# Input projections of a hybrid attention and GLA layer by a seven-product scheme, with attention and GLA as side work

## The chip, the core and the metric

The kernel runs on one core of a Trainium2 chip. A core has a matrix engine (TensorE, PE in the profile; its weight loads are listed as PEld), a vector engine (VectorE, DVE), a scalar engine (ScalarE, ACT), a general engine (GpSimd, POOL) and a queue engine that issues transfers (SyncE, SP). Each engine works through its own instructions in order and waits on semaphores for the others. The metric is device time in microseconds from the first to the last instruction of one execution, with inputs and outputs in device memory (DRAM).

## What is computed

One layer of a decoder on 2048 prompt tokens and 8 x 8 new tokens (2112 in all), 1024 wide, in single precision. One input matrix gives eleven projections. Sliding-window attention (blocks of 128 tokens, each seeing itself and the block before) and a gated linear attention (GLA, 4 heads, a recurrent state carried from chunk to chunk) are computed from them, gated, projected and merged; an output projection and a layer normalisation follow. Cut to its core:

```python
z = jnp.einsum('btd,dn->btn', x, w_in)
q, k, v, g_att, gq, gk, gv, g_gla, g_lr, r_att, r_gla = jnp.split(z, SPLIT_POINTS, axis=-1)
o_att = swa_prompt(q, k, v, attn_sink, rel_table)          # or swa_sample, with the caches
log_a = log_sigmoid(g_lr @ w_gk_up + b_gk) / 16
o_gla, S = gla(gq * HK ** -0.5, gk, gv, log_a, s0)         # per chunk, with b = cumsum(log_a):
    # S = exp(b_last) * S + (k * exp(b_last - b)).T @ v
    # o = (q * exp(b)) @ S_before + causal((q * exp(b)) @ (k * exp(-b)).T) @ v
o_gla = o_gla * rsqrt(mean(o_gla ** 2) + EPS) * gla_norm_w
h_att = (o_att * silu(g_att)) @ w_pa
h_gla = (o_gla * silu(g_gla)) @ w_pg
y = (sigmoid(r_att) * h_att + sigmoid(r_gla) * h_gla) @ w_o
x = layer_norm(DN_ALPHA * x + y, ln_g, ln_b)
```

The widths of the projections are q 512, k 128, v 128, g_att 512, gq 512, gk 512, gv 1024, g_gla 1024, g_lr 16, r_att 1024, r_gla 1024. Outputs besides x are the last keys and values and the GLA states.

## The kernel before

Every large product runs at near single precision as three matmuls of a faster operand type: both factors are split into a high part (a rounded copy, made by ACT) and a low part (the remainder, by default made by DVE), and high x high, high x low and low x high are summed in PSUM. `split`, lines 114 to 118, is this pair of instructions; its lines 115 and 116 stand for nearly all splits in the profile.

The kernel has four stages.

1. *Attention*, six chunks of tokens (`CHUNKS`: four of 384, one of 256, one of 256 + 64 samples). For each chunk the ten 128-column tiles of k, v, q and g_att are projected by `proj` (lines 176 to 187, eight slices of the 1024-wide sum by three matmuls, the chunk's tokens streaming), the 16 gate columns by lines 638 and 639. The x tiles are split once per chunk (`part_x`; from the second chunk on, POOL makes every second low part). Attention of the blocks of the chunk runs as side work: functions are put into a list of time slots with `at`, and `tick`, called after each projection, runs those of the next slot (`att_scores`, `att_trans`, `att_out`). The results go to `ua_d` in DRAM.
2. *GLA*, four heads by the same six chunks. x is loaded and split again for each head. k, q and the two gate tiles go through `proj`, the values through `proj_t` (lines 189 to 200, x stationary, 256 value columns streaming, so that the values come out with tokens on the partitions). `gla_z`, `gla_a`, `gla_b`, `gla_c` are the side work of a block of 128 tokens, placed by `chain`. Sums of x tiles that the later passes need ("combinations", `combine_load` and `combine_do`, four additions each) are made here too.
3. *Four passes* by a seven-product scheme (Strassen's in Winograd's form): `w_pa`, `w_ra`, `w_rg`, `w_pg`. A pass treats its product as a 2 x 2 block product (two halves of the sum, and pairs of 352-token groups and of 128-column tiles), with seven block products in place of eight (`ORDER`, `combine`). A *unit* is one of the seven products for one of three token pairs (`MS`); a *group* is a unit's 128-column tile `p`, twelve matmuls of 352 columns (six in w_pa), lines 1276 to 1278. `prep_w` makes sums of weight tiles on POOL and splits them; `prep_x` splits the x sums, 1408 wide; `combine` adds the product to the accumulators on DVE (lines 1123 to 1140), with one addition on POOL (line 1130); a sink stores the finished tile. Nothing else runs beside these passes except the last combinations and early loads of w_o.
4. *Output projection and layer norm* (`Rows`), tiles of 128 tokens.

The order on PE is the order of the program text. The other engines' instructions are put in order by a planner that ranks them by program order and modelled readiness. Tiles come from pools of fixed numbers of buffers; PSUM has three banks `pd` for projections and five `pa` for side work and for the passes.

Of the kernel before, what the change touches and what calls it, by code (L numbers as in the profile page):

```python
# [21 lines left out]
P = 128  # L22
# [19 lines left out]
CHUNKS = [(0, 384), (384, 384), (768, 384), (1152, 384), (1536, 256), (1792, 320)]  # L42
# [4 lines left out]
NU = 29  # L47
NX = 20
# [3 lines left out]
def kernel(ctx, tc, io):  # L52
# [4 lines left out]
    phase = ctx.enter_context(ExitStack())  # L57
    sb = phase.enter_context(tc.tile_pool(name="sb", bufs=1, reuse_waits="tile"))
# [3 lines left out]
    ctx.enter_context(tc.manual_schedule(engines={mybir.EngineType.PE}))  # L62

# [8 lines left out]
    def wtile(dt=F32, name="w"):  # L72
        return sb.tile([P, D], dt, tag="w", name=name, bufs=26)

    def stile(name):
        return sb.tile([P, D], F32, tag="s", name=name, bufs=2)

    def unit(dt=F32, name="u"):
        return sb.tile([P, TM], dt, tag="u", name=name, bufs=NU)

    def small(shape, name, bufs=3):
        return sb.tile(shape, F32, tag=name, name=name, bufs=bufs)

    ua_d = dram.tile([P, 4, NT], F32, name="ua_d")
# [35 lines left out]
    wseq = [0, 10]  # L120
    wready = deque()
    pin = {}

    def wload(n=1):
        for _ in range(n):
            i = wseq[0]
            if i >= wseq[1]:
                return
            wseq[0] += 1
            st = sb.tile([P, D], F32, tag="wst", name="wst", bufs=2)  # L130
            pin["w"] = nc.sync.dma_start(st, io["wt"][i])
            hi = wtile(F32R, "wh")
            lo = wtile(F32R, "wl")
            split(hi, lo, st)
            wready.append((hi, lo))

    def wget():
        if not wready:
            wload()
        return wready.popleft()  # L140

    def xnew():
        return sb.tile([P, TM], F32R, tag="x", name="x", bufs=NX)

    def xstage():
        return sb.tile([P, TM], F32, tag="xst", name="xst", bufs=4)

    def fetch(src, k, t0, T, stage=xstage):
        st = stage()
        nc.sync.dma_start(st[:, :T], src[:, k, t0:t0 + T])  # L150
        return st, T

    def part(f, new=xnew, eng=nc.vector, samples=False):
        st, T = f
        hi, lo = new(), new()
        split(hi[:, :T], lo[:, :T], st[:, :T], eng)
        if samples:
            nc.gpsimd.tensor_copy(hi[:, T:T + NS], lo[:, T - NS:T])
        return hi, lo

    def load_split(src, k, t0, T, new):
        return part(fetch(src, k, t0, T), new)

    def fetch_x(src, t0, T):

        return [fetch(src, k, t0, T, unit if k < KT // 2 else xstage) for k in range(KT)]

    def part_x(fs, share=False, samples=False):

        return [part(f, eng=nc.gpsimd if share and k % 2 else nc.vector, samples=samples)  # L170
                for k, f in enumerate(fs)]

    def load_x(src, t0, T, stage=xstage, samples=False):
        return [part(fetch(src, k, t0, T, stage), samples=samples) for k in range(KT)]

    def proj(ps, w, x, T, mid=False):

        hi, lo = w
        n = len(x)
        for k in range(n):  # L180
            if mid and k == n // 2:
                tick()
            s = slice(k * P, (k + 1) * P)
            xh, xl = x[k]
            mm(ps, hi[:, s], xh[:, :T], start=(k == 0), stop=False)  # L185
            mm(ps, hi[:, s], xl[:, :T], start=False, stop=False)  # L186
            mm(ps, lo[:, s], xh[:, :T], start=False, stop=(k == n - 1))  # L187

    def proj_t(ps, x, c0, n, w, N, cs=slice(None)):

        per = D // N
        for k in range(KT):
            hi, lo = w[k // per]
            r = slice((k % per) * N, (k % per + 1) * N)
            hi, lo = hi[:, r][:, cs], lo[:, r][:, cs]
            xh, xl = x[k]
            xs = slice(c0, c0 + n)
            mm(ps, xh[:, xs], hi, start=(k == 0), stop=False)  # L198
            mm(ps, xl[:, xs], hi, start=False, stop=False)  # L199
            mm(ps, xh[:, xs], lo, start=False, stop=(k == KT - 1))  # L200

    def proj_s(ps, dst, x, c0, w, N, cs=slice(None)):


        per = D // N
        for k in range(KT):
            hi, lo = w[k // per]
            r = slice((k % per) * N, (k % per + 1) * N)
# [324 lines left out]
    def wcap(n):  # L533
        wseq[1] = n
# [381 lines left out]
    for h in range(GH):  # L916
        W2 = {}
        wcap(16 + 6 * h)
        for c, (t0, T) in enumerate(CHUNKS):
# [81 lines left out]
            x = xn  # L1001

# [482 lines left out]
```

## Time and profile before

| what | value |
|---|---|
| median of 3 runs | 1837.22 us (1836.84 to 1837.51) |
| profiled execution, its span | 1836.5 us |
| profiled execution, its own time around the span | not given by the page |
| PE, PEld, DVE, ACT, POOL busy | 98%, 94%, 70%, 46%, 23% of the span |
| mean granted TensorE clock | 0.994 |
| memory read, written | 229.05 MB, 86.14 MB; 172 GB/s over the span |

The profile of one execution says how long each engine was busy, groups instructions by program line with their mean duration, and follows the chain of work that ended last. Matmuls overlap in the array and their ends are modelled, so the mean duration of a matmul is longer than the interval at which matmuls follow each other; the interval is read from start times. A timeline row gives start, duration, engine, line, operation, output and inputs, and a count where like instructions were merged. A row of a stretch gives its length and then, for each engine, busy time and the number of instructions.

### The profile page before, as it was taken

To read this page: it belongs to the slowest core of one execution; us is meant where nothing else is said; L and a number is where in the kernel's file an instruction comes from. 1 tells how busy PE (TensorE), PEld (TensorE's weight loads), DVE (VectorE), ACT (ScalarE), POOL (GpSimd) and SP (SyncE) were. 2 spreads that over 40 slices of the span, in tenths; PEclk is the share of its full clock that TensorE was granted. 3 is DMA by queue.
4 is the path that set the end of the run, shared out by engine and by line. 5 is a ranking of instruction groups with operands and counts; after the bars stand their busy time and mean duration, and the time that the engine had idled before them with its cause. 6 is when DMAs were issued, how large, how long until landed. Compare 5 with 4: busy or idle time off the path is not lost.

```text
span 1836.5 us, 32287 instructions
## 1 busy us (share of the span) xinstructions
PE 1805.2 (98%) x11683; PEld 1718.5 (94%) x11683; DVE 1282.0 (70%) x2663; ACT 850.2 (46%) x1948; POOL 421.9 (23%) x559
## 2 busy tenths in 40 slices
PE   8999999999999999999999999999999999999997
PEld 7988988899999999999999989999999999988886
DVE  6686778767776776777667669748756576966655
ACT  5444545645665664656555553444543443220110
POOL 3310111300110111011110233430355163631111
PEclk9999999999999999999999999999999999999998
DMA  7111013544345444533543189858887967884531
GB/s 243 54 56 38 13 46 100 166 132 156 122 149 168 141 140 153 187 127 112 168 158 122 57 267 316 296 185 281 284 311 256 340 221 265 287 305 142 169 115 41
DMA packets 199408, 316.34 MB, mean 172 GB/s; under 512 B 20797, under 2 KB 161045, under 8 KB 199232
## 3 DMA queue, kind: packets, MB, share of 16 engines
q1 hardware_dynamic: 193536, 306.57, 50.9%
q0 software_dynamic: 5616, 7.58, 1.5%
q8 instruction: 92, 1.51, 0.3%
q14 instruction: 68, 0.56, 0.1%
q10 hardware_dynamic: 96, 0.13, 0.0%
HBM read 229.05 MB, written 86.14 MB: 172 GB/s over the span
## 4 chain that ended last, share of the span: by engine, by line
PE 91%; DMA 2%; DVE 2%; issue 2%; POOL 1%; ACT 1%; SPq 0%; DVEq 0%; POOLq 0%; ACTq 0%
PE pd L185 11%; PE pd L187 11%; PE pd L186 11%; PE pa L1276 9%; PE pa L1278 9%; PE pa L1277 9%; PE pd L199 7%; PE pd L200 7%; PE pd L198 7%; PE pa L421 2%; PE pa L406 1%; PE pa L754 1%; PE pa L755 1%; PE pa L753 1%; POOL a L1159 1%
## 5 line engine op out<-in xcount | busy, mean ns | idle before, releaser
L185 PE MATMUL pd<-x,wh 128*128 128x384 f32 (+2 forms) x1248 | 409.7, 328 | 5.6 <-ACT x L115 5.6
L186 PE MATMUL pd<-x,wh 128*128 128x384 f32 (+2 forms) x1248 | 404.2, 324 | 0.4 <-POOL x L116 0.2
L187 PE MATMUL pd<-x,wl 128*128 128x384 f32 (+2 forms) x1248 | 403.5, 323 | 0.6 <-DVE wl L116 0.6
L1277 PE MATMUL pa<-xl,wh 128*128 128x352 f32 x1168 | 376.1, 322 | 3.6 <-DVE xl L116 3.3
L1276 PE MATMUL pa<-xh,wh 128*128 128x352 f32 x1168 | 377.1, 323 | 0.9 <-ACT a L1120 0.9
L1278 PE MATMUL pa<-xh,wl 128*128 128x352 f32 x1168 | 376.5, 322 | 0.0
L185 PEld LDWEIGHTS pd<-x,wh 128*128 128x128 f32 x1248 | 236.7, 190 | 15.6 <-issue 8.9
L186 PEld LDWEIGHTS pd<-x,wh 128*128 128x128 f32 x1248 | 236.9, 190 | 1.9 <-DVE x L116 1.4
L187 PEld LDWEIGHTS pd<-x,wl 128*128 128x128 f32 x1248 | 236.6, 190 | 1.0 <-DVE wl L116 1.0
L1277 PEld LDWEIGHTS pa<-xl,wh 128*128 128x128 f32 x1168 | 219.4, 188 | 6.1 <-DVE xl L116 6.1
L1276 PEld LDWEIGHTS pa<-xh,wh 128*128 128x128 f32 x1168 | 219.0, 187 | 2.1 <-ACT a L1120 1.1
L1278 PEld LDWEIGHTS pa<-xh,wl 128*128 128x128 f32 x1168 | 220.9, 189 | 0.0
L116 DVE TENSOR_TENSOR xl<-xs,xh 128x1408 fp32r<-128x1408 f32 x63 | 111.4, 1769 | 73.1 <-ACT xh L115 42.8
L198 PE MATMUL pd<-wh,x 128*128 128x256 f32 x512 | 147.8, 289 | 0.0
L199 PE MATMUL pd<-wh,x 128*128 128x256 f32 x512 | 145.6, 284 | 0.6 <-POOL x L116 0.3
L200 PE MATMUL pd<-wl,x 128*128 128x256 f32 x512 | 144.6, 282 | 0.0
L115 ACT CAST x<-xst 128x384 fp32r<-128x384 f32 (+2 forms) x164 | 77.5, 484 | 143.4 <-PE pd L199 112.3
L115 ACT CAST xh<-xs 128x1408 fp32r<-128x1408 f32 x63 | 86.5, 1373 | 98.5 <-PE pa L1278 80.9
L746 POOL TENSOR_SCALAR sq<-sq 128x1 f32<-128x1 f32 (+1 forms) x68 | 21.7, 319 | 467.2 <-ACT ring L745 467.1
L198 PE MATMUL pd<-woh,x 128*128 128x512 f32 x256 | 102.1, 399 | 4.2 <-ACT x L115 4.2
L199 PE MATMUL pd<-woh,x 128*128 128x512 f32 x256 | 102.3, 400 | 0.2 <-DVE x L116 0.2
L200 PE MATMUL pd<-wol,x 128*128 128x512 f32 x256 | 102.0, 398 | 0.0
(345 smaller groups left out, 3695.4 us busy)
## 6 DMA issues: line engine op xcount, KB each, us to landing
wst<-wt SPq DMA_DIRECT2D x33, 512.0 KB, 3.6
xs<-xc_d SPq DMA_DIRECT2D x24, 704.0 KB, 5.7
u<-xT SPq DMA_DIRECT2D x84, 192.0 KB, 4.0
xst<-xT SPq DMA_DIRECT2D x76, 192.0 KB, 2.7
xs<-xT SPq DMA_DIRECT2D x18, 704.0 KB, 6.2
ws<-w_ra SPq DMA_DIRECT2D x36, 256.0 KB, 4.4
ws<-w_rg SPq DMA_DIRECT2D x36, 256.0 KB, 5.1
ws<-w_pg SPq DMA_DIRECT2D x36, 256.0 KB, 5.1
```

The lines of the kernel that those rows point to most:

```text
L115: pin["a"] = nc.scalar.copy(dst_h, src)
L116: i = eng.tensor_tensor(dst_l, src, dst_h.bitcast(F32), ALU.subtract)
L185: mm(ps, hi[:, s], xh[:, :T], start=(k == 0), stop=False)
L186: mm(ps, hi[:, s], xl[:, :T], start=False, stop=False)
L187: mm(ps, lo[:, s], xh[:, :T], start=False, stop=(k == n - 1))
L198: mm(ps, xh[:, xs], hi, start=(k == 0), stop=False)
L199: mm(ps, xl[:, xs], hi, start=False, stop=False)
L200: mm(ps, xh[:, xs], lo, start=False, stop=(k == KT - 1))
L421: mm(ot[pr, :], vb[:, pr], A["pT", bi, kv][:, hf], start=(hf == h0), stop=(hf == 1))
L1276: mm(ps, wh[:, ks], xh[:, ts], start=(k == 0), stop=False)
L1277: mm(ps, wh[:, ks], xl[:, ts], start=False, stop=False)
L1278: mm(ps, wl[:, ks], xh[:, ts], start=False, stop=(k == q.kh - 1))
```

## The change

Stages 1 to 3 become one list of eight seven-product passes over all 2112 tokens: attention (`w_at`, five pairs of column tiles, so five groups a unit), three GLA passes (`w_g0` to `w_g2`, together k and q, values and gates of the four heads, four groups a unit), then `w_pa`, `w_ra`, `w_rg`, `w_pg` as before. Every projection is written to DRAM by a sink (`z_kv`, `z_q`, `z_ga`, `z_kq`, `z_vv`, `z_gg`; the gates after their silu). Attention and GLA read them back and run as side work of later passes: attention in chunks of 256 tokens beside the first GLA pass, one block in five ticks; the GLA chains of the four heads one after another from the second GLA pass to twelve ticks before `w_pg`. A tick follows every group (every second one in `w_pa`). The combinations of x move into the attention pass, together with the product for the 16 gate columns, now from unsplit tiles in four 32-column tiles of PE. In the GLA passes the low part of x is made by POOL. The values arrive with channels on the partitions and are transposed on PE (`gla_v`). PSUM has four banks for products and four for side work. The output stage is unchanged. The diff, cut to its core ("a5", "ws5" and the like are the fifth pair's tiles, from other pools):

```diff
-CHUNKS = [(0, 384), (384, 384), (768, 384), (1152, 384), (1536, 256), (1792, 320)]
+AT = 256
+GT = 256
+NW4 = 10
...
-    psd = ctx.enter_context(tc.tile_pool(name="psd", bufs=3, space=PSUM))
-    psa = ctx.enter_context(tc.tile_pool(name="psa", bufs=5, space=PSUM))
+    psd = ctx.enter_context(tc.tile_pool(name="psd", bufs=4, space=PSUM))
+    psa = ctx.enter_context(tc.tile_pool(name="psa", bufs=4, space=PSUM))
...
+        def prep_x(self, i, s, x):
+            hl = [mtile("xb", F32R, n)[:, :self.kh * T] for n in ("xh", "xl")]
+            split(*hl, x, self.eng)
+            return hl
...
+    def keep_sink(dst):
+        def f(z, parts, p, c, ts):
+            nc.sync.dma_start(dst[:, c, ts], z)
+            wrote(dst, c, ts)
+        return f
+    def silu_sink(dst, scale=None):
+        def f(z, parts, p, c, ts):
+            th = mtile("fin", name="th")
+            nc.scalar.activation(th, z, AF.Tanh, scale=0.5)
+            if scale is not None:
+                nc.scalar.mul(z, z, scale[:, c:c + 1])
+            nc.vector.scalar_tensor_tensor(z, th, 1.0, z, ALU.add, ALU.mult)
+            nc.sync.dma_start(dst[:, c, ts], z)
...
+    passes = [Pass(io["w_at"], 4, 5, xT, xc_d, [keep_sink(z_kv)] + [keep_sink(z) for z in z_q] +
+                   [silu_sink(z) for z in z_ga])]
+    passes += [Pass(io[f"w_g{j}"], 4, 4, xT, xc_d, gsinks[4 * j:4 * j + 4], eng=nc.gpsimd) for j in range(3)]
+    passes += [Pass(io["w_pa"], 2, 4, ua_d, ac_d, [store_sink] * 4),
+               Pass(io["w_ra"], 4, 4, xT, xc_d, [gated_sink] * 4, parts=ha_d),
+               Pass(io["w_rg"], 4, 4, xT, xc_d, [gate_sink] * 4),
+               Pass(io["w_pg"], 4, 4, None, uc_d, [merge_sink] * 4, parts=tt_d)]
...
+    def xcombo(s, k, eng):
+        x1, x2, dst, last = cx.pop((s, k))
+        if k == 0:
+            glp[s] = pa()
+        for j, x_ in enumerate((x1, x1, x2, x2)):
+            r = slice(32 * j, 32 * j + 32)
+            mm(glp[s][r, :T], wg[:, k + 4 * (j // 2), :], x_[:, j % 2 * T:(j % 2 + 1) * T], start=(k == 0),
+               stop=(k == 3), tile_position=(0, 32 * j))
+        combine_do(x1, x2, dst, last, eng)
...
+    for j in range(12):
+        at(1 + 1.5 * j, xload)
+        at(8 + 1.5 * j, lambda j=j: xcombo(j // 4, j % 4, nc.vector))
...
+    SB = 5
+    for c in range(NP // AT):
+        b0 = ta + 14 + c * 2 * SB
+        at(b0 - 12, lambda c=c: att_load(c))
+        at(b0 - 5, lambda c=c: att_prep(c))
+        for g in range(G):
+            at(b0 - 4 + g // 2, lambda c=c, g=g: att_queries(c, g))
+        at(b0 - 1, lambda c=c: att_sil(c))
+        for bi in range(2):
+            o = b0 + bi * SB
+            at(o, lambda c=c, bi=bi: att_scores(c, bi, 0))
+            at(o + 1, lambda c=c, bi=bi: att_scores(c, bi, 1))
+            at(o + 4, lambda c=c, bi=bi: att_trans(c, bi, 0))
+            at(o + 5, lambda c=c, bi=bi: att_trans(c, bi, 1))
+            at(o + 7, lambda c=c, bi=bi: att_out(c, bi))
...
+    def gla_v(B, i):
+        ...
+        for m in range(2):
+            nc.tensor.transpose(tp[:n, m * P:(m + 1) * P], B["zvv"][:, m, ts], ident)
+        v = tp[:n, :HV]
+        split(gh[:n], gl[:n], v)
...
+    tg = max(tick_of(P_G1) + 2, t_att + 3)
+    t_end = tick_of(P_PG) - 12
+    HS = (t_end - tg - 14) / GH
+    ST = (HS - 4) / (NP // P)
+    for h in range(GH):
+        chain(h, tg + 14 + h * HS, ST)
...
+        issue_x(n + 2)
+        if n:
+            issue_x(n + 3)
+        issue_w(n + 1)
+        make_x(n + 1)
+        make_w(n)
+        for p in range(q.np):
+            ...
+            ps = (pa() if n >= UPG + 6 and g % 2 else pd())[:, :T]
+            for k in range(q.kh):
+                mm(ps, wh[:, ks], xh[:, ts], start=(k == 0), stop=False)
+                mm(ps, wh[:, ks], xl[:, ts], start=False, stop=False)
+                mm(ps, wl[:, ks], xh[:, ts], start=False, stop=(k == q.kh - 1))
+            q.combine(i, p, s, ps, parts.get(g))
+            half[0] += 1
+            if q.kh == 4 or half[0] % 2 == 0:
+                tick()
```

With passes of 105, 84, 84, 84, 42, 84, 84 and 84 ticks, attention starts near tick 117 and ends near 208, the GLA chains run from tick 225 to about 555, each block of 128 tokens in 4.9 ticks, and `w_pg` starts at tick 567.

More of the change, by code (lines that the diff above doesn't have):

```diff
@@ L137, in wget @@
[L137 to L200, printed above, removed]
@@ new lines, with tick_of @@
+    P_AT, P_G0, P_G1, P_G2, P_PA, P_RA, P_RG, P_PG = range(8)
+    units = [(q, i, s) for q in passes for i in ORDER for s in range(MS)]
+    UP = len(ORDER) * MS
+    groups = [(n, q, i, s, p) for n, (q, i, s) in enumerate(units) for p in range(q.np)]
+    first_group = {}
+    for g, (n, *_) in enumerate(groups):
+        first_group.setdefault(n, g)
+    def tick_of(j):
+        t = 0
+        for q in passes[:j]:
+            t += UP * q.np // (2 if q.kh == 2 else 1)
+        return t
+    plan = {n: [] for n in range(-2, len(units))}
@@ new lines, in make_x, with issue_parts @@
+    def make_x(n):
+        if n < len(units) and n not in xp:
+            q, i, s = units[n]
+            xp[n] = q.prep_x(i, s, xs.pop(n))
+    def issue_parts(g):
+        if g < len(groups) and g not in parts:
+            n, q, i, s, p = groups[g]
+            parts[g] = q.partners(i, p, s)
+    combos = {"x": deque((xT, xc_d, 4, k, s) for s in range(MS) for k in range(4)),
+              "a": deque((ua_d, ac_d, 2, k, s) for s in range(MS) for k in range(2)),
+              "u": deque((None, uc_d, 4, k, s) for k0 in (0, 2) for s in range(MS) for k in (k0, k0 + 1))}
@@ new lines, in combo @@
+    def combo(key, eng):
+        combine_do(*combine_load(combos[key].popleft()), eng)
+    mpool("c0")
+    q0 = passes[0]
+    raws[0, 0] = q0.raw_w(1, 0)
+    x0 = mtile("xb", F32, "xs")
+    hl0 = [mtile("xb", F32R, n) for n in ("xh", "xl")]
+    for k in range(4):
+        ts = slice(k * T, (k + 1) * T)
+        nc.sync.dma_start(x0[:, ts], xT[:, k, toks(0, 0)])
+        if k == 0:
+            wts[0, 0] = q0.prep_w(1, 0, raws.pop((0, 0)))
+        split(hl0[0][:, ts], hl0[1][:, ts], x0[:, ts])
@@ L1163 @@
-    passes = [Pass(io["w_pa"], 2, ua_d, ac_d, [], store_sink),
-              Pass(io["w_ra"], 4, io["xT"], xc_d, [ha_d], gated_sink),
-              Pass(io["w_rg"], 4, io["xT"], xc_d, [], gate_sink),
-              Pass(io["w_pg"], 4, None, uc_d, [tt_d], merge_sink)]
-    units = [(q, i, s) for q in passes for i in ORDER for s in range(MS)]
-    groups = [(q, i, s, p) for q, i, s in units for p in range(NP4)]
-    plan = {n: [] for n in range(-2, len(units))}
-    for n in range(0, len(units), MS):
-        q, i, _ = units[n]
-        for p in range(NP4):
-            plan[max(n - MS + MS * p // NP4, -1)].append((n, q, i, p))
```

1255 lines of the change are left out of this document (582 added, 673 removed).

## The prediction

> **What bounds the kernel now.** I read the totals first, then the chain that ended last, then busy time by stretch, and last the start times of single instructions, because modelled matmul ends hide how densely TensorE (PE) is fed.
>
> ```profile
> span 1836.5 us, 32287 instructions
> PE 1805.2 (98%) x11683; PEld 1718.5 (94%) x11683; DVE 1282.0 (70%) x2663; ACT 850.2 (46%) x1948; POOL 421.9 (23%) x559
> ...
> PE 91%; DMA 2%; DVE 2%; issue 2%; POOL 1%; ACT 1%; SPq 0%; DVEq 0%; POOLq 0%; ACTq 0%
> ...
> core 0: us, PE busy (x) PEld busy (x) DVE busy (x) ACT busy (x) POOL busy (x), PEclk, DMA share, GB/s
> 0.00:31.00 31.00, 24.47 (x111) 21.60 (x111) 19.74 (x31) 18.61 (x33) 8.34 (x25) 0.99 0.64 202
> 125.54:187.52 61.98, 61.98 (x382) 55.99 (x380) 43.99 (x108) 26.70 (x83) 5.44 (x11) 1.00 0.14 42
> 395.60:568.00 172.40, 172.36 (x1244) 170.00 (x1242) 121.07 (x312) 99.29 (x243) 23.03 (x50) 1.00 0.49 155
> 1127.00:1280.00 153.00, 152.98 (x957) 152.85 (x957) 111.02 (x164) 69.35 (x108) 40.05 (x29) 1.00 0.80 262
> 1280.00:1434.00 154.00, 154.00 (x964) 154.00 (x963) 100.93 (x135) 72.46 (x116) 66.65 (x52) 1.00 0.83 289
> 1434.00:1470.00 36.00, 36.00 (x227) 36.00 (x226) 21.30 (x29) 18.14 (x29) 8.35 (x6) 1.00 0.98 338
> ```
>
> PE carries 91% of the chain. The stretches are: the start, one steady attention chunk (three blocks of 128 tokens), one GLA head (16 blocks), the w_ra pass, most of the w_rg pass, and the densest DMA stretch. PE never idles in the middle ones, so PE work removed there is time removed. But VectorE (DVE) is already busy 71% of the attention chunk (43.99 of 61.98) and 70% of a GLA head, and the change shrinks PE's share of exactly those stretches.
>
> **What PE gains.** The interval between matmul starts is what counts.
>
> ```profile
> L185 PE MATMUL pd<-x,wh 128*128 128x384 f32 (+2 forms) x1248 | 409.7, 328 | 5.6 <-ACT x L115 5.6
> L198 PE MATMUL pd<-wh,x 128*128 128x256 f32 x512 | 147.8, 289 | 0.0
> ...
> 86.48 0.34 PE L187 MATMUL pd<-x,wl 128*128 128x384 f32 x1
> ...
> 89.97 0.33 PE L186 MATMUL pd<-x,wh 128*128 128x384 f32 x1
> 391.81 0.28 PE L200 MATMUL pd<-wl,x 128*128 128x256 f32 x1
> ...
> 393.25 0.28 PE L200 MATMUL pd<-wl,x 128*128 128x256 f32 x1
> 1299.77 0.32 PE L1278 MATMUL pa<-xh,wl 128*128 128x352 f32 x1
> ...
> 1305.85 0.32 PE L1277 MATMUL pa<-xl,wh 128*128 128x352 f32 x1
> ```
>
> Twenty intervals of 384 columns take 3.49 us, 0.174 each; twelve of 256 take 1.44, 0.120 each; thirty-eight of 352 take 6.08, 0.160 each. 320 columns lie between, at 0.147. The old projections are 3 x 1248 matmuls, of which four chunks in six are 384 wide, one 256, one 320: 3 x (832 x 0.174 + 208 x 0.120 + 208 x 0.147) = 601 us. The values add 3 x 512 x 0.120 = 184, and their sample rows 64 matmuls, 8. Together 793 us. New: the attention pass has 7 products x 3 token pairs x 5 tiles x 12 matmuls = 1260, the three GLA passes 1008 each; 4284 x 0.160 = 685. **Gain 108 us.** The pass is counted in ticks, one per group of 12 matmuls, 1.92 us.
>
> PE work added or moved:
>
> ```profile
> 90.48 0.87 PE pa L406 x8
> 547.87 1.85 PE pa L830 x16
> ...
> 1061.13 6.08 DMA ug_d<-sg
> ```
>
> The values now arrive transposed: 4 heads x 17 blocks x 2 transposes x 0.109 (0.87 / 8) = **+15 us**. The low-rank gate becomes 48 full-precision matmuls of 352 columns in 32-wide column tiles. Line 830 is the same kind: 8 calls (two records each) in 1.85 us, 0.231 for 256 columns, so 0.318 for 352 and 15 us; before it was 96 of 0.12 to 0.174, also 15. **Zero.** The other attention and GLA matmuls move unchanged: 5.8 us a block ((61.98 - 240 x 0.174 - 16 x 0.174) / 3) and about 2.0 a GLA block. The later passes keep their matmuls. The GLA tail no longer drains in front of w_pa, where PE waited at most the 6.08 us of that store; I credit none, since early products filled part of it. PE alone: 1836.5 - 108 + 15 = 1743.5.
>
> **The start.** By tick 25 PE needs twelve x combinations (8.65 MB loaded, 7.9 of it stored again), eight x units (5.8) and twenty weight tiles (5.2), 27.5 MB. At the 338 GB/s of the densest stretch that is 81 us; PE has 5 + 25 x 1.92 + 15 = 68. The old start lost 6.5 (31.00 - 24.47). Net **+7**, between -6 (no wait) and +20. Later stages stay below 338: w_ra's 262 x 153 us is 40 MB, 17 GLA blocks add 10 MB, over a pass that grows to 199 us: 251 GB/s.
>
> **Queues.** SP gets about 200 stores of z, 260 reads of it, and 120 more weight loads, and loses some 160 x loads: +420.
>
> ```profile
> 1299.66 0.43 SPq L1151 DMA_DIRECT2D tt_d<-a  x1
> xs<-xT SPq DMA_DIRECT2D x18, 704.0 KB, 6.2
> ```
>
> At 0.43 that is 181 us of issuing spread over 1100. A store that waits for DVE holds the x loads behind it, but an x load lands in 6.2 us and is issued two to three units (15 to 23 us) ahead. Cost nothing; without that cover, the lateness of DVE is added per unit. Moving the product banks from the pool of five to one of four costs nothing while DVE drains a bank within three groups, 5.8 us.
>
> **What DVE and POOL (GpSimd) take back.** In the GLA passes (not the attention pass) POOL computes the low part of x, 1408 wide, 21 times a pass.
>
> ```profile
> L1123 DVE TENSOR_TENSOR fin<-a,pa 128x352 f32<-128x352 f32 x44 | 22.3, 512 | 9.7 <-PE pa L1278 6.0 <-DMA tt_d<-fin 3.4 <-PE pa L1277 0.4
> L116 DVE TENSOR_TENSOR x<-u,x 128x384 fp32r<-128x384 f32 x78 | 41.1, 552 | 4.4 <-ACT x L115 3.7
> L116 DVE TENSOR_TENSOR wl<-wst,wh 128x1024 fp32r<-128x1024 f32 x33 | 40.5, 1229 | 8.1 <-ACT wh L115 7.2 <-issue 0.3
> L863 DVE TENSOR_TENSOR x<-x,x 128x352 f32<-128x352 f32 x24 | 12.4, 516 | 0.0
> L221 DVE SCALAR_TENSOR_TENSOR sg<-th,pd 128x384 f32<-128x384 f32 x32 | 17.6, 549 | 10.3 <-ACT th L220 10.3
> L115 ACT CAST xh<-xs 128x1408 fp32r<-128x1408 f32 x63 | 86.5, 1373 | 98.5 <-PE pa L1278 80.9 <-DMA xs<-uc_d 16.6 <-DMA tt_d<-a 0.9
> L116 POOL TENSOR_TENSOR x<-u,x 128x384 fp32r<-128x384 f32 x6 | 6.7, 1121 | 100.2 <-ACT x L115 100.1
> L116 POOL TENSOR_TENSOR x<-u,x 128x256 fp32r<-128x256 f32 x2 | 1.5, 748 | 46.8 <-ACT x L115 46.8
> L1055 POOL TENSOR_TENSOR ws<-ws 128x512 f32<-128x512 f32 x12 | 16.9, 1406 | 126.9 <-ACT a L1149 36.6 <-DMA ha_d<-a 26.7 <-DMA ws<-w_pg 22.1
> L1130 POOL TENSOR_TENSOR a<-a,a 128x352 f32<-128x352 f32 x44 | 50.9, 1174 | 50.6 <-DVE a L1129 50.4
> ...
> 1303.96 0.51 DVE L1140 TENSOR_TENSOR a<-a,pa 128x352 f32<-128x352 f32 x1
> 1304.93 1.12 POOL L865 TENSOR_TENSOR xc<-xc 128x352 f32<-128x352 f32 x1
> 1305.16 1.44 DVE L116 TENSOR_TENSOR wl<-ws,wh 128x512 fp32r<-128x512 f32 x1
> ...
> 1308.14 0.68 DVE L116 TENSOR_TENSOR wl<-ws,wh 128x512 fp32r<-128x512 f32 x1
> ...
> 133.96 1.14 DVE L396 TENSOR_SCALAR s<-s,rd 128x256 f32<-128x256 f32 x4
> 247.76 2.11 DVE L396 TENSOR_SCALAR s<-s,rd 128x256 f32<-128x256 f32 x4
> 248.19 0.77 POOL L116 TENSOR_TENSOR x<-u,x 128x256 fp32r<-128x256 f32 x1 [13.16 <-ACT x L115]
> ```
>
> POOL grows 0.0029 us a column (1.121 - 0.748 over 128), so 1408 take 4.1 us; with 16 weight sums (1.4) and 12 product sums (1.17) a pass has 122 us of POOL in 84 ticks, 1.46 a tick. While POOL works, a DVE operation that reads SBUF twice doubles (0.68 to 1.44), the softmax scaling nearly so (1.14 to 2.11 for four), and an add from PSUM does not (0.51).
>
> *Attention* runs over 80 ticks beside the first GLA pass, a block every five. PE: 5 x 1.92 + 5.8 = 15.4 us a block. DVE: the chunk's 43.99 less four x splits and four gates at about 0.55 is 39.6, 13.2 a block; the pass adds per tick 72/84 adds (0.512), 28/84 weight splits (0.68) and 12/84 gates (0.55), 0.74, less some overlap 0.66: 3.3. That is 16.5, **1.1 over PE, 18 us in 16 blocks**. If the 6 us of DVE work that POOL doubles meet POOL for its 43% of the time, 2.4 more: 18.9, 56 us. The 2.11 row is this very operation under POOL, so I take a value nearer the upper end, **+40**.
>
> [...]
>
> *GLA* runs one block in 4.9 ticks, from the second GLA pass into w_rg. PE: 4.9 x 1.92 + 2.0 + 0.2 = 11.6 a block. DVE: the head's 121.07 less 48 x splits (0.55), 6 weight splits (1.23), 6 combinations of four (0.516 each) and 12 gates (0.55), 53 us, some 50 without their overlap, is 71, 4.4 a block; with 3.6 of the pass 8.0, up to 10.6 under POOL. Beside the two GLA passes that hides: **+3**, 0 to 25. In w_ra PE has 161 + 17 x 2.2 = 199 and DVE 111 + 17 x 4.4 = 186; in w_rg 194 and 101 + 65 + 13 for six combinations = 179. At 93% busy some waits reach PE: **+13** with w_pa, 0 to 40.
>
> **Sum.** 1743.5 + 7 + 40 + 3 + 13 = 1806.5 of the profiled execution's span. The page gives no time around the span; the runs' median, 1837.22, is 0.7 above it, so 1807.
>
> **Rivals.** *DVE hides all it can*: POOL and DVE seldom meet, attention costs 18, the rest nothing: 1743.5 + 0 + 18 = 1762. For it speaks that PE did not idle at 71% DVE; against it the 2.11 row.
>
> *POOL's x split comes late* (the other side). xl of the next unit can start only when PE has left the previous one: cast 1.4, split 4.1, and in front of it weight or product sums; a unit is 7.7 us of PE, 9.5 beside GLA. If DVE slows POOL by 1.4 (a 352-wide POOL sum would take 1.03 by the slope and is at 1.12 and above), 1.4 + 5.7 + two sums of 1.2 is 9.5: at the edge. Each microsecond over costs 63 us in 63 units; from 0.5 us (30 / 63) the kernel is slower than before. I price it at 0.7 a unit, 44: 1851. [...]
>
> *DVE saturates everywhere*: attention 56, GLA 25 and 40, start 10 and a little more: within 4 us of before.
>
> **Chances.** Forecast 0.48 (1780 to 1830), hidden 0.22, late split or saturation beyond 0.24, no change 0.06. A difference of 0.2%, 3.7 us, is about what a measurement can tell. Faster 0.48 + 0.22 = 0.70, same 0.06, slower 0.24. The forecast's terms at both ends give 1756 and above 1870; with one case in ten left out on either side the range is 1755 to 1850.
>
> **What would show it.** PE matmul starts 0.160 us apart in the new passes. Attention steps of about 18 us for five ticks with DVE over 95% busy and PE waiting for score or transposed-weight copies on DVE. The weight split at 1 us or more beside POOL. A first 80 us with DMA near 338 GB/s. Wrong would be: PE waiting for xl from POOL in many units; DVE below 90% during attention; w_ra and w_rg much longer than 199 and 194 us.

## The result, and the profile after

The changed kernel takes 1987.95 us (median of 4 runs, 1982.41 to 1992.59) against 1837.37 (1836.84 to 1842.19) for the kernel before: 1.0809 times, 95% interval 1.0784 to 1.0834. It is **8% slower**, where 1807 us was forecast. The profiled execution's span is 1980.6 us.

The page after: totals, the granted clock in forty slices, the chain that ended last.

```profile
span 1980.6 us, 31502 instructions
PE 1794.6 (91%) x10771; PEld 1669.9 (84%) x10771; DVE 1532.7 (77%) x2872; ACT 978.5 (49%) x2139; POOL 716.5 (36%) x604
...
PEclk9799999999899989999999899999998999999999
...
PE 41%; DVE 25%; DMA 13%; ACT 8%; POOL 6%; issue 5%; SPq 1%; DVEq 0%; POOLq 0%; ACTq 0%
```

PE's part of the chain fell from 91% to 41%. PE is no longer the bound. The same by stage: attention pass, three GLA passes, w_pa, w_ra, w_rg, w_pg (columns as before).

```profile
4.60:254.60 250.00, 228.17 (x1376) 212.59 (x1377) 160.93 (x240) 80.66 (x127) 76.69 (x82) 0.95 0.80 269
254.60:569.40 314.80, 269.68 (x1583) 237.44 (x1582) 281.06 (x548) 171.04 (x460) 102.83 (x50) 0.93 0.49 155
569.40:792.30 222.90, 209.17 (x1401) 197.63 (x1399) 181.00 (x344) 127.57 (x278) 123.30 (x86) 0.97 0.72 228
792.30:1033.90 241.60, 212.62 (x1319) 203.72 (x1317) 189.89 (x370) 152.13 (x337) 115.38 (x86) 0.96 0.56 175
1033.90:1160.90 127.00, 112.20 (x674) 105.28 (x672) 103.66 (x251) 77.00 (x186) 30.54 (x42) 0.93 0.71 224
1160.90:1383.80 222.90, 206.97 (x1315) 201.78 (x1316) 191.44 (x411) 150.79 (x332) 59.83 (x65) 0.96 0.77 242
1383.80:1610.60 226.80, 203.67 (x1279) 197.51 (x1279) 173.40 (x341) 134.58 (x292) 88.43 (x88) 0.95 0.81 270
1610.60:1783.60 173.00, 165.53 (x1016) 164.18 (x1015) 127.62 (x178) 57.14 (x80) 86.95 (x69) 0.98 0.83 282
```

No stage keeps PE fed, and the clock, 0.99 to 1.00 in the old stretches, is at 0.93 to 0.98. What PE waited for (total, times, longest):

```profile
PE pa L623 <- DVE s L612: 35.3, 20, 5.0
PE pd L1160 <- ACT xh L144: 20.7, 6, 5.8
PE pa L967 <- ACT ring L933: 14.9, 8, 4.2
PE pd L1161 <- DVE xl L145: 14.8, 7, 6.3
PE pa L938 <- ACT ak L144: 10.5, 9, 2.9
PE pa L940 <- DVE ak L145: 10.5, 10, 2.0
...
PE pd L1161 <- POOL xl L145: 5.2, 3, 4.0
```

All rows of this view sum to 176.3 us, 18.2 before: +158. The clock record has 33 episodes at half rate, 172 us of the span (before: 3, 21 us). In 135 us of them PE has work (before: 10); matmuls then come 0.29 us apart in place of 0.160 (shown below), so about half of the 125 more is lost, an estimated 60. Together 218, and the span is 237 above the 1743.5 that the prediction gave PE alone; the 19 left stand in neither row. So **the forecast's PE time nearly holds, and the loss is waits of PE, and the half-rate clock that follows them**.

### The profile page after: what moved, and what is told of

Same layout as the page of the kernel before. It is cut to its first block, busy times and chain, and to the rows that moved or that the text cites. A ratio compares the mean times of both kernels' runs of the same rounds, so it can differ in the third digit from the quotient of the medians.

```text
span 1980.6 us, 31502 instructions
## 1 busy us (share of the span) xinstructions
PE 1794.6 (91%) x10771; PEld 1669.9 (84%) x10771; DVE 1532.7 (77%) x2872; ACT 978.5 (49%) x2139; POOL 716.5 (36%) x604
## 4 chain that ended last, share of the span: by engine, by line
PE 41%; DVE 25%; DMA 13%; ACT 8%; POOL 6%; issue 5%; SPq 1%; DVEq 0%; POOLq 0%; ACTq 0%
PE pd L1160 9%; PE pd L1161 9%; PE pd L1162 8%; PE pd L1207 3%; PE pd L1206 3%; PE pd L1205 3%; DVE wl L145 2%; DVE s L612 2%; ACT xh L144 2%; DVE xl L145 2%; DMA ws<-w_g 2%; DMA ws<-w_at 1%; DVE nm L603 1%; POOL a L243 1%; DVE s L600 1%
## 5 line engine op out<-in xcount | busy, mean ns | idle before, releaser
L1160 PE MATMUL pd<-xh,wh 128*128 128x352 f32 x2484 | 842.3, 339 | 39.2 <-ACT xh L144 20.7
L1161 PE MATMUL pd<-xl,wh 128*128 128x352 f32 x2484 | 817.9, 329 | 20.1 <-DVE xl L145 14.8
L1162 PE MATMUL pd<-xh,wl 128*128 128x352 f32 x2484 | 816.2, 329 | 0.0
L1160 PEld LDWEIGHTS pd<-xh,wh 128*128 128x128 f32 x2484 | 482.6, 194 | 67.7 <-issue 22.8
L1161 PEld LDWEIGHTS pd<-xl,wh 128*128 128x128 f32 x2484 | 484.1, 195 | 23.9 <-DVE xl L145 17.7
L1162 PEld LDWEIGHTS pd<-xh,wl 128*128 128x128 f32 x2484 | 482.4, 194 | 0.0
L145 POOL TENSOR_TENSOR xl<-xs,xh 128x1408 fp32r<-128x1408 f32 x63 | 207.8, 3298 | 234.0 <-ACT xh L144 227.2
L144 ACT CAST xh<-xs 128x1408 fp32r<-128x1408 f32 (+2 forms) x171 | 218.2, 1277 | 109.5 <-PE pd L1161 93.6
L145 DVE TENSOR_TENSOR wl<-ws,wh 128x512 fp32r<-128x512 f32 (+1 forms) x231 | 190.9, 835 | 71.7 <-ACT wh L144 59.5
L145 DVE TENSOR_TENSOR xl<-xs,xh 128x1408 fp32r<-128x1408 f32 (+2 forms) x108 | 170.5, 1580 | 46.7 <-ACT xh L144 45.6
L931 POOL TENSOR_SCALAR sq<-sq 128x1 f32<-128x1 f32 (+1 forms) x68 | 32.3, 476 | 260.6 <-ACT ring L930 260.6
L933 ACT ACTIVATE ring<-pa,sq 128x256 f32<-128x256 f32 (+1 forms) x68 | 32.3, 474 | 118.0 <-POOL sq L932 118.0
```

Of the source, the lines that this page charges most:

```text
L144: pin["a"] = nc.scalar.copy(dst_h, src)
L145: i = eng.tensor_tensor(dst_l, src, dst_h.bitcast(F32), ALU.subtract)
L1160: mm(ps, wh[:, ks], xh[:, ts], start=(k == 0), stop=False)
L1161: mm(ps, wh[:, ks], xl[:, ts], start=False, stop=False)
L1162: mm(ps, wl[:, ks], xh[:, ts], start=False, stop=(k == q.kh - 1))
```

## What the half-rate clock costs

In the trace after, each of the 15 gaps on PE of 3.1 us or more has an episode in it or right behind it, and one stands within 5 us of 14 of the 18 of 2.0 to 3.0. Shorter gaps are mixed: four episodes stand behind a single gap of 1.4 to 2.0 us, and eight other gaps of 1.2 to 2.0 have none. To see whether the wait causes it, waits were put into the passes w_ra and w_rg of the kernel before, which has no episode there (the edit in short):

```diff
+ if w_ra or w_rg, and g % 8 == 0 (second kernel: g % 4 == 0):
+     nc.tensor.transpose(pw[:, :P], ident, ident)
+     nc.scalar.copy(stw, pw[:, :P])
+     for _ in range(13):                       # second kernel: 5
+         nc.scalar.copy(stw, stw)
+     nc.tensor.transpose(pw[:, P:2 * P], stw, ident)
```

> The kernel before (1837 us) with 21 waits of PE put into w_ra and w_rg, one every eight groups, each behind a chain of 14 small ACT copies (about 4.5 us). Without an effect on the clock the time grows by the waits alone, 21 x 4.5 = 95, or what the trace shows them to be. Theory 'a wait of over 3 us halves the clock for 3.4 to 10 us afterwards': 21 half-rate episodes appear where there were none, and 36 to 70 us come on top.

> The kernel before with 42 waits of PE in the same two passes, one every four groups, each behind 6 small ACT copies (about 2.1 us), so about the same sum of waits, 90 us. Theory 'only long waits halve the clock': few or no half-rate episodes, the time grows by the waits alone. If the clock follows the sum of idle time and not the single wait, as many episodes appear as with the long waits.

2019.04 us (1.0986, 1.0953 to 1.1018) and 2066.40 us (1.1244, 1.1214 to 1.1274). The waits came out longer than meant. PE's row for them in the waits of the long kernel, and in those of the short one:

```profile
PE pa L1281 <- ACT stw L1280: 131.1, 21, 6.6
```

```profile
PE pa L1281 <- ACT stw L1280: 151.1, 42, 4.0
```

Busy time in four stretches of the long kernel: before one wait, the wait, 5 us behind it, and 10 us later (the clock is the third figure from the right):

```profile
1140.50:1154.00 13.50, 13.50 (x85) 13.50 (x85) 10.58 (x16) 6.30 (x9) 2.59 (x2) 1.00 1.00 333
1154.00:1160.50 6.50, 0.35 (x4) 0.07 (x2) 1.88 (x1) 5.75 (x16) 3.05 (x3) 0.91 1.00 363
1161.00:1166.00 5.00, 5.00 (x19) 5.00 (x19) 0.00 (x0) 0.45 (x1) 3.54 (x4) 0.50 0.72 271
1167.00:1177.00 10.00, 10.00 (x65) 10.00 (x64) 2.92 (x3) 4.83 (x9) 2.07 (x2) 1.00 0.27 68
```

The clock is 0.50 behind the wait: 19 matmuls in 5 us, 0.29 apart, for 0.160. All 21 waits of 6.2 us are followed by 6.8 us at half rate, part of it inside the wait; 35 of the 42 waits of 3.6 us by 3.4 or 6.8 us. The seven without one are 3.2 to 3.6 long, so length alone doesn't decide. The span grew by 182.4 us; less 131.1 of waits and 4.6 for 42 transposes (0.109 each), 46.7 are left, **2.2 us a wait**, about half of the 90 us more in which PE works at half rate. With the shorter waits 225.2 - 151.1 - 9.2 = 64.9, **1.5 a wait**. That waits cause the episodes is shown: the mean granted clock is 0.960 and 0.964 in these two kernels, 0.994 before. The rate at which short ones do isn't: the second kernel missed its size of 2 us. Nor is there one length that divides them: 21 of 21 waits of 6.2 us had an episode, seven of 3.2 to 3.6 us had none, and in the changed kernel 14 of the 18 gaps of 2 to 3 us, and four below, sufficed.

## Where the waits come from: the passes alone

Attention and GLA left out, then GLA alone left out (the edits in short).

```diff
- at(...) of setup, att_load ... att_out, samp_*, gla_load ... gla_c      # first kernel: all
+ gates loaded and stored unchanged                                       # second: gla_* only
```

> Leaves out attention and all GLA chains: the gates of attention are passed on unchanged, the GLA gates are stored unchanged, and the key, value and state outputs are not written. What is left is the eight passes with their combinations and the output stage. The sum from the rows: 7812 matmuls x 0.160 = 1250, gate matmuls 15, output stage 197, start 7 to 15, about 1475 us. If the passes by themselves are slow (POOL's split of x late, or loads late at the start), it stays above 1550, with PE waiting for xl. If the loss lies in the side work, it is 1460 to 1500, the clock stays near 1, and side work costs about 510 us in the changed kernel where its PE work is about 93 (attention) + 170 (GLA).

> Leaves out the GLA chains only (their gates are loaded and stored unchanged; GLA state outputs not written); attention stays beside the first GLA pass. Theory 'DVE and POOL in attention': that pass keeps its 315 us (PE content 161 + 93 + samples), the total is about 1475 + 155 = 1630, and the other passes run at 168 to 173 us each. Rival 'GLA chains disturb everything, even the first GLA pass': that pass falls below 290. What GLA costs is then 1988 - 1630 = 358 us, where its PE work is about 170.

1614.63 and 1765.02 us (one run each). The bare passes take 140 us more than the sum, the case named as passes slow by themselves: **a loss of 140 us needs no side work at all**, and the second total misses by 135. The pass beside attention keeps its length, 318 us, so GLA doesn't disturb it. Attention then adds 150 us (1765 - 1615) where its PE work was put at 93, and GLA 223 (1988 - 1765) where its PE work was put at 170: beyond PE's work 57 and 53, less than the passes lose alone. In the bare kernel PE's waits sum to 105.6 us, with 100 us at half rate; the three largest:

```profile
PE pd L1125 <- POOL xl L145: 38.6, 17, 5.7
PE pd L1124 <- DVE a L242: 14.8, 5, 8.2
PE pd L1124 <- ACT xh L144: 12.9, 5, 4.6
```

Then the same bare passes with the low part of x on DVE (`eng=nc.gpsimd` taken out of the three GLA passes).

> Leaves out attention and GLA as in the kernel without side work, and has the low part of x made by DVE in the three GLA passes. Theory 'POOL's split comes late in the bare passes': the 38.6 us of PE waiting for that split and the half-rate clock behind it go; the three GLA passes fall from 186 + 179 + 182 to about 165 to 170 each, the total from 1614.6 to about 1575; the other stages keep their losses (attention pass about 243, w_pa 97, w_ra 182). Rival 'the wait is for the x load or the buffers, whoever splits': DVE's split waits as long and the total stays above 1605.

1580.96 us (one run); the three passes 174, 167, 167. The 34 us go with POOL's split: its lateness and what it does to DVE (next section) are not separated here. Part of the gain went back at once: PE now waits 29.6 us, in six waits, for DVE additions (8.7 with the split on POOL); three of these additions waited 22.5 us for tiles that were not yet stored.

## POOL's split

The same edit in the whole kernel, and POOL's split cut in four:

```diff
- passes += [Pass(io[f"w_g{j}"], ..., gsinks[4 * j:4 * j + 4], eng=nc.gpsimd) for j in range(3)]
+ passes += [Pass(io[f"w_g{j}"], ..., gsinks[4 * j:4 * j + 4]) for j in range(3)]
```

```diff
- i = eng.tensor_tensor(dst_l, src, dst_h.bitcast(F32), ALU.subtract)
+ for k in range(4):
+     cs = slice(k * T, (k + 1) * T)
+     eng.tensor_tensor(dst_l[:, cs], src[:, cs], dst_h[:, cs].bitcast(F32), ALU.subtract)
```

> The low part of x in the three GLA passes made by DVE in place of POOL. Theory 'DVE is saturated by load': DVE gets 63 operations of some 1.7 us, 107 us; the attention pass, where DVE is 90% busy, grows by 25 to 36 us, the others by less: 2010 to 2050. Theory 'POOL's long operations hold DVE': the other DVE operations shorten (wl from 835 toward 700 ns, softmax scaling from 557 toward 380) and waits for the norm's POOL steps behind the split fall; the first GLA pass stays or shrinks (at most 315), the other two shrink by 10 to 30 each: 1900 to 1970.

> POOL's split of x as four operations of 352 columns in place of one of 1408: same work on the same engine. Theory 'a DVE operation that meets POOL is held until POOL's operation ends': a DVE operation is held at most 0.9 us and small POOL steps can slip between: wl below 780 ns, total 1920 to 1970. Theory 'DVE merely runs at half rate under POOL, so only the load counts': within 10 us of the changed kernel, 1978 to 1998.

1922.71 us (1.0453, 1.0404 to 1.0502) and 1969.34 (1.0714, 1.0678 to 1.0749). DVE got 110 us more of its own work, its busy time yet fell from 1532.7 to 1501.9 us, and the kernel became **65 us faster**. Two groups of DVE in the changed kernel, then in the one with the split on DVE (busy us and mean ns behind the first bar):

```profile
L612 DVE TENSOR_SCALAR s<-s,rd 128x256 f32<-128x256 f32 x120 | 56.6, 533 | 0.5
L604 DVE TENSOR_TENSOR nm<-nm,nsink 128x4 f32<-128x4 f32 x32 | 11.2, 349 | 0.1
```

```profile
L612 DVE TENSOR_SCALAR s<-s,rd 128x256 f32<-128x256 f32 x120 | 38.3, 382 | 0.5
L604 DVE TENSOR_TENSOR nm<-nm,nsink 128x4 f32<-128x4 f32 x32 | 4.9, 154 | 0.1
```

Three encounters in the timeline of the changed kernel, POOL's row above DVE's:

```profile
291.16 3.23 POOL L145 TENSOR_TENSOR xl<-xs,xh 128x1408 fp32r<-128x1408 f32 x1
291.49 2.92 DVE L609 TENSOR_TENSOR es<-es,sm 128x4 f32<-128x4 f32 x1 [0.85 <-ACT es L608]
...
405.25 3.20 POOL L145 TENSOR_TENSOR xl<-xs,xh 128x1408 fp32r<-128x1408 f32 x1 [1.74 <-ACT xh L144]
406.66 1.81 DVE L604 TENSOR_TENSOR nm<-nm,nsink 128x4 f32<-128x4 f32 x1
...
537.72 3.38 POOL L145 TENSOR_TENSOR xl<-xs,xh 128x1408 fp32r<-128x1408 f32 x1 [1.21 <-ACT xh L144]
537.94 3.18 DVE L607 TENSOR_TENSOR es<-sink,nm 128x4 f32<-128x4 f32 x1
```

Four elements a partition take 0.15 to 0.26 us in the mean where POOL has no split, and 1.8 to 3.2 here, and the ends agree: 291.49 + 2.92 = 294.41 against 294.39, 408.47 against 408.45, 541.12 against 541.10. All 17 operations of lines 604, 607 and 609 that start while POOL works end 15 to 25 ns after POOL's. Wider ones are held too: eleven weight splits (128x512, 0.68 us alone) that start well inside POOL's split take 1.75 to 3.67 us and end 0.55 after it. Additions that read PSUM and one tile of SBUF aren't: the 20 of lines 236 to 253 that start inside the split take 0.50 to 0.52. **These DVE operations with two inputs in SBUF aren't slowed, they are held until POOL's is done**, and the profile counts the time held as busy (2.92 us in the first encounter). The prediction's own row says it, read again: 1305.16 + 1.44 = 1306.60, POOL was done at 1306.05, and the 0.55 left is what the eleven show. What in the chip holds them no run shows. With the quarters the holds are shorter: the scaling's mean falls from 533 to 469 ns, the time by 19 us. How much of the 65 us is the hold, and how much the lateness of the split for PE, was not separated.

## Beside attention: DVE's load, not pace or lag

```diff
- SB = 5                       att_prep at b0 - 5; att_trans at o + 4, o + 5; att_out at o + 7
+ SB = 6                       att_prep at b0 - 3; att_trans at o + 5, o + 6; att_out at o + 8
```

> The kernel with the split on DVE with an attention block every six ticks in place of five, transposes one tick later. The GLA chains start 16 ticks later and get less time. DVE per block is 16.5 to 18.9 us by the prediction; a block then has 6 x 1.92 + 4.1 = 15.6 us of PE. Theory 'DVE's load': the loss beside attention (59 us over PE's work in the first GLA pass, plus a part in the second) falls to 20 to 30 and the GLA passes lose 5 to 10: 1880 to 1905. Theory 'the chain of one block (scores, softmax, transposes) is simply longer than the lag': about the same. If neither, the total stays at 1915 to 1930.

1933.35 us (1.0506, 1.0488 to 1.0524): nothing gained. A block takes 19.7 us in the changed kernel (mean of 15 intervals between its first score matmuls), 18.3 with the split on DVE, 19.6 at six ticks a block. PE's own work in a block is 15.4 us at five ticks and 6 x 1.92 + 5.8 = 17.3 at six, so a block is 2.9 over it at five and still 2.3 at six: a slower pace gives little back. Now take work from DVE:

```diff
- nc.vector.tensor_scalar(s[:, g, k0:], s[:, g, k0:], rd[:, g:g + 1], None, op0=ALU.mult)
+ nc.scalar.mul(s[:, g, k0:], s[:, g, k0:], rd[:, g:g + 1])
- if hf: nc.vector.tensor_copy(pT[:, hf], tp)
- else: nc.scalar.copy(pT[:, hf], tp)
+ nc.scalar.copy(pT[:, hf], tp)
```

> The kernel with the split on DVE (1923 us), with the softmax scaling (four DVE operations a head group) and the copies of transposed weights moved from DVE to ACT, some 4 us of DVE a block of 128 tokens; ACT goes from 0.61 to about 0.8 of the time beside attention. Theory 'in attention DVE's load sets the pace': a block needs 15.5 to 16.5 us in place of 18.4, PE then sets it, and the first GLA pass falls from 286 to 245 to 260: total 1885 to 1900. Rival 'latency of the chain over engines': ACT's copies come as late as DVE's did, and the total stays within 10 us of 1923.

1900.64 us (1.0340, 1.0299 to 1.0381). Busy time in 200 us of steady attention, in the changed kernel, with the split on DVE, and in this one:

```profile
300.00:500.00 200.00, 168.98 (x991) 145.11 (x992) 188.54 (x377) 111.61 (x308) 59.78 (x28) 0.94 0.46 144
```

```profile
300.00:500.00 200.00, 179.95 (x1092) 155.26 (x1091) 191.18 (x428) 122.88 (x336) 16.31 (x15) 0.96 0.52 162
```

```profile
300.00:500.00 200.00, 191.73 (x1173) 161.64 (x1172) 170.20 (x342) 176.30 (x476) 20.68 (x18) 0.99 0.57 178
```

By the move to ACT alone DVE falls from 96% to 85%, PE rises from 180 to 192 us, and a block takes 17.0 in place of 18.3. Load, then. But ACT is at 88% now, and the pass is 269 us, not the 245 to 260 expected.

## The GLA stages: a chain over three engines

Later calls of the second and third steps of a block, alone and with the slower attention (the split on DVE in both; the last steps of a chunk move along):

```diff
- at(o + 3, ... gla_b(B, i));  at(o + 7, ... gla_c(B, i, P, i * P))
+ at(o + 5, ... gla_b(B, i));  at(o + 11, ... gla_c(B, i, P, i * P))
```

> The kernel with the split on DVE (1923 us) with later second and third steps of each GLA block (state step five ticks after the first in place of three, output step eleven in place of seven). Theory 'latency: the steps are called before their operands are through ACT and DVE': PE's waits in these steps (about 40 us) mostly go and the half-rate clock behind them too: 1860 to 1895. Theory 'load: DVE cannot do the work in the time': the waits move to other steps and the total stays at 1910 to 1930.

> Both of the last two edits together, on the kernel with the split on DVE. If both gains are real and separate they add up: 1820 to 1870; if one takes from the other (GLA chains with less time and longer lags), 1870 to 1900.

1935.87 us (1.0526, 1.0508 to 1.0543) and 1917.40 (1.0429, 1.0405 to 1.0453). The first lost 13 us, nearest to the theory of load: PE's waits sum to 147 us in place of 140, and stand at other steps. The second is within the noise of 1923 where 50 to 100 us were expected. Next, DVE's load in the passes over x, first by keeping the split tiles in DRAM, then by not making the low part:

```diff
+ for j in range(2): nc.sync.dma_start(xk_d[i, s, :, j], hl[j])   # first time; later loaded, not split
```

```diff
- split(*hl, x, self.eng); return hl
+ nc.scalar.copy(xh, x); return [xh, xh]                          # w_g0 to w_g2, w_ra, w_rg
```

> The kernel with the split on DVE, in which the split x tiles (both parts) are stored in DRAM when they are first made (15 of the 21 in the attention pass, six in the first GLA pass) and loaded in place of being split again in the five later passes over x: about 95 casts of 1.37 us on ACT and as many splits of 1.74 us on DVE go, 1.44 MB a unit are loaded in place of 0.72. Theory 'load of DVE (and the cast-split chain)': PE waits less in all five passes, 33 to 36 us of DVE less in each; 1840 to 1880. Rival 'transfers become the bound' (47 to 60 MB in a pass of 200 us, 240 to 300 GB/s against the 344 seen): no gain, 1900 to 1950, with PE waiting for loads of x.

> The kernel with softmax scaling on ACT (1900 us). In the five passes over x that are not the attention pass the low part of x isn't made; the high part stands in for it, so that PE's work is the same and DVE is spared about 36 us a pass, with no transfer more. Theory 'DVE's load in the GLA stages': the first GLA pass falls from 269 to about 240, the next two from 210 and 213 to about 200, w_ra and w_rg from 224 and 227 to 200 to 208: total about 1800 to 1830. Rival 'waits across engines in the GLA chain (ACT, POOL, DVE in turn), whatever DVE's load': w_ra and w_rg stay above 217, total above 1860.

1959.78 us (1.0660, 1.0630 to 1.0690), 37 slower: 532 MB moved in place of 431, and PE waits for the gate inputs' loads (`PE pa L873 <- DMA gin<-gl_d`, 53.3 us in nine waits, up to 17.2). That is nearest to the rival, which had named loads of x; whether the rate or the order of the transfers made these loads late is open. Without the low part 1860.03 (one run), between the two theories: 269 to 253, 210 to 204, 213 to 210, w_ra 224 to 213, w_rg 227 to 227. A block of attention takes 15.8 us, PE's own 15.4. So DVE's load, together with the shorter way from cast to product, is 40 us in all, but **not what holds w_rg**, where DVE is busy 63%. Two last tries on this kernel: the later calls again, and the norm without POOL (the block scaled by a constant):

```diff
- nc.gpsimd.tensor_scalar(sq[:n], sq[:n], EPS, None, op0=ALU.add)
- nc.gpsimd.tensor_tensor(sq[:n], sq[:n], mhalf[:n], ALU.pow)
- nc.scalar.mul(on[:n], o, sq[:n])
+ nc.scalar.mul(on[:n], o, mhalf[:n])
```

> The kernel in which the low part of x isn't made in five passes (1860 us; the high part stands in for it), with the later second and third steps of each GLA block that gave nothing while DVE was loaded (1923 to 1936). Theory 'a chain over several in-order engines needs slack in load and in calling time together': now the waits at the state step and the output step (some 20 us with their half-rate clock) go, w_ra 213 to 203 to 207, w_rg 227 to 208 to 215, total 1825 to 1840. Rival 'the single long waits in w_ra and w_rg come from somewhere else (sums, transfers) and move to the next step called': total within 10 us of 1860.

> The same kernel (1860 us) without POOL's two small steps in the norm of a GLA block: the block is scaled by a constant, so that the chain ACT, POOL, POOL, ACT ahead of the output step is ACT alone. Theory 'the norm's chain over POOL holds the output step': the waits for the scaled block and for the gates after it (5 us in w_rg, more in the other kernels) go and w_rg falls to about 215, total 1835 to 1850. Rival as above: 1850 to 1870, the waits being at the state step.

1867.56 and 1822.36 us (one run each). Calling later does nothing, even with DVE relieved. Two small POOL operations a block, some 61 us of POOL in all, cost **38 us of the kernel**. ACT's row for them in its waits, in the changed kernel and in the one without the low part:

```profile
ACT ring L933 <- POOL sq L932: 118.0, 60, 7.3
```

```profile
ACT ring L934 <- POOL sq L933: 101.0, 63, 7.0
```

ACT stands still 1.6 to 2 us a block, up to 7, for a number per row, and in its queue behind that stand the casts of the states, of x and of the weights, for which DVE's low parts and then PE wait: that is how I read it; what is shown is the 38 us. POOL's queue stands at the same place while it waits for ACT's sum (`POOL sq L932 <- ACT ring L931`, 333.2 us in 41 waits), and which of the two queues costs the time is not separated. The kernel before has the same two steps; ACT stood 53.4 us for them in 59 waits, up to 1.6, and PE hardly waited. In the last kernel ACT's row is gone, w_ra takes 203.5 us (199 forecast), w_rg 220.

## The start, and SP's queue

Sums of x tiles made 50 ticks later (the attention pass reads plain x for four products); then the stores of all sums on another queue:

```diff
- at(1 + 1.5 * j, xload);   at(8 + 1.5 * j, ... xcombo ...)
+ at(51 + 1.5 * j, xload);  at(58 + 1.5 * j, ... xcombo ...)
```

```diff
- nc.sync.dma_start(dst[n_:n_ + 2]...)
+ nc.gpsimd.dma_start(dst[n_:n_ + 2]...)        # second kernel: nc.scalar
```

> The kernel with softmax scaling on ACT (1900 us), with the sums of x tiles made 50 ticks later; the attention pass reads plain x tiles for the four products that would need them, so it loads as much for its products but not the 16.5 MB of making the sums within the first 25 ticks. Theory 'the start is bound by transfers': the waits for x in the first 110 us (25 us) and the three half-rate episodes behind them go, the attention pass falls from 250 to 225 to 232, total about 1875 to 1882. Rival 'DVE's additions and splits or the buffers make x late at the start': the attention pass stays above 243.

> The kernel with softmax scaling on ACT (1900 us), in which the 60 stores of sums of x tiles are issued by POOL's queue in place of SP's; nothing else is moved. In w_rg of the changed kernel SP stood still from 1463.5 to 1471.3 us behind such a store that waited for additions, and PE waited 10 us for the x load behind it. Theory 'stores that wait for an engine hold the x loads on SP': the waits for x at the start and in w_rg and w_pg go, and the half-rate clock behind them: attention pass 250 to about 242, w_rg 227 to 210 to 215, w_pg 175 to 168: total 1860 to 1880. Rival 'transfers are late by themselves': 1890 to 1910.

> The same 60 stores issued by ACT's queue in place of SP's. By the theory of the queue the x loads are free as well, but now a store that waits for an addition holds ACT's casts of x and w behind it: between the kernel with the stores on POOL's queue and 1900; if it is slower than 1900, the cost has only moved to ACT's queue.

1894.75 (one run), 1901.86 (1.0348, 1.0324 to 1.0371) and 1898.02 us (1.0336, 1.0306 to 1.0366). With the sums late, the attention pass falls from 250 to 242, a third of what transfers were expected to give: PE still waits 9 us for casts of x. It lies between the two theories, near the rival's 243, and the total is within the spread of the kernel without the edit (1892 to 1908); what else makes the start late stays open. For the queue, the timeline of SP in w_rg of the changed kernel (L204 loads x, L376 stores sums), then PE's two waits in it:

```profile
1463.17 0.32 SPq L204 DMA_DIRECT2D xs<-xc_d  x1
1471.33 1.54 SPq L376 DMA_DIRECT2D uc_d<-x  x2
...
1480.87 0.51 SPq L204 DMA_DIRECT2D xs<-xc_d  x1
```

```profile
1487.83 0.66 PE L1160 MATMUL pd<-xh,wh 128*128 128x352 f32 x1 [5.13 <-ACT xh L144]
...
1493.00 0.66 PE L1161 MATMUL pd<-xl,wh 128*128 128x352 f32 x1 [4.51 <-DVE xl L145]
```

SP stood for 8 us at a store that waited for sums, then worked off thirteen other transfers, and the x load came at 1480.87, too late. The kernel with scaling on ACT, on which these edits stand, has the same two waits (4.4 and 4.9 us). With the stores elsewhere the first is gone from w_rg and the second falls to 1.2 and 2.4, but the stage stays at 227 to 229 and the totals don't move from 1901: PE's waits at the GLA output step grow from 5.6 to 10.9 and 12.6 us. The attention pass takes 254 and 244 us, 250 without the edit, where about 242 was expected: no clear gain there either. That curing one wait shows the next is how I read it.

## Why the prediction was wrong

The kernels above, each standing on the one before, take the loss apart (the last two leave work of DVE or POOL out and are one run each):

| kernel | us | step |
|---|---|---|
| changed | 1988 | |
| low part of x on DVE | 1923 | -65 |
| softmax scaling on ACT | 1901 | -22 |
| low part not made | 1860 | -41 |
| norm without POOL | 1822 | -38 |

- **PE's gain: right.** Matmuls of 352 columns follow each other at 0.160 us wherever PE is fed and at full clock, and the last kernel, with the same work on PE, ends at 1822. Its span is 77 us above 1743.5; its waits are 56 above those of before and its half-rate clock is worth about 20, so nothing is left over.
- **The passes alone, nothing but the start's +7: wrong, and the largest part.** They lose 140 us without any side work. By stage, over 0.160 us a matmul and with the start: 26 in the attention pass, 25, 18 and 21 in the GLA passes with POOL's split, and 17, 21, 6 and 13 in the four later ones, where PE waits mostly for DVE's additions. The failed step is taking a full PE in the last passes of before as a full PE in all eight.
- **The start, +7: its estimate was right, its price too low.** Tick 25 was put at 81 us and began at 80.2. Beyond it waits went on to 104 us (25 us of waits in the pass, 27 us at half rate).
- **Attention, +40: right in kind, short in size.** DVE is 94% busy and PE waits for the softmax scaling, as forecast; a block takes 19.7 us, not 17.9, so 16 x (19.7 - 15.4) = 69. The failed step is "doubles": in the changed kernel a hold lasts until POOL's operation ends (to 25 ns in 17 of 17 small operations). With the split on DVE, 2.2 us more of DVE's work a block, a block takes 18.3, near the sum 16.5 + 2.2: the load was sized rightly, the meeting with POOL was not. POOL's split itself took 3.3 us and not 4.1.
- **GLA, +3 and +13: wrong.** The two GLA passes took 223 and 242 us against 199 each (84 ticks and 17 blocks), 67 where +3 was forecast; with the split on DVE 214 and 217. w_ra and w_rg took 223 and 227 against 199 and 194, though DVE's load was nearly as forecast (191 and 173 us against 186 and 179). The failed step is weighing only DVE's busy share. A block's steps go through ACT, DVE and POOL in turn, and a step late on any of them reaches PE: less load on DVE brought w_ra to 213 and w_rg nothing, the norm without POOL 203.5 and 220. In the passes alone w_ra already lost 21 us and w_rg 6, and what holds w_rg at 220 is open.
- **Queues, nothing: wrong in its bound.** In w_rg the x load was late as the prediction described, once, for 10 us. Moving the stores gave nothing back; other waits grew.
- **PSUM banks, nothing:** PE waits for DVE or ACT to empty banks (`DVE a L247` and the like) some 16 us in all; small.
- **The rival "POOL's x split comes late"** was priced at 44 us and measured 34 in the bare passes. In the whole kernel PE waits only 5.2 us for it directly, so the list's "PE waiting for xl from POOL in many units" did not show; that its cost came through the held DVE is argued from the timeline and the quarters. One sign of being wrong on the list did: w_ra and w_rg much longer than 199 and 194.
- **The clock: not in the sum at all.** An estimated 60 us, over a third as much again as the waits that bring it. In the stretches quoted of before the clock stood at 0.99 to 1.00, as PE hardly waited there.

The rival "DVE saturates everywhere" named the right direction and stopped at its bounds; the sum of all bounds was exceeded by causes that it did not hold.

## What to carry to other kernels

PE of the kernel before hardly waited (18.2 us in all) while the others had slack (DVE was 70% busy); before PE is made faster, count the slack of every in-order queue that a step passes through, not the busiest engine alone, and build the new stages without their side work first, to see what they lose alone. Here a wait of PE of 3.6 or 6.2 us cost a third to a half as much again in clock. Keep wide POOL operations away from a DVE that reads two tiles of SBUF (here splits of 3.3 us held it), and don't send a value through POOL in the middle of a chain that ACT's queue waits for (118.0 us of waits here).

None of the complete kernels here beats the one before; the best is 3.4% slower.

## What was not expected of the hardware

- Small DVE operations that take 0.15 us alone and up to 3.18 us beside a POOL operation, ending 15 to 25 ns after it in 17 of 17 cases, while additions from PSUM ran through in 0.50 to 0.52 us.
- PE at half clock for 3.4 to 10.2 us behind waits of mostly 2 to 6.3 us: 32 episodes in one execution and one behind its last matmul, and 21 of 21 where waits of 6.2 us were put in.
- The 338 GB/s of one stretch of before, taken as the start's rate, gave tick 25 to within 1 us (341 measured over the first 80 us, though 379 from 20 to 60 us).
